# A short FFN part: two of its down blocks as a pair of seven products, and later joins of the query rows, in a float32 decoder layer on one core

## The chip, the cores and the metric

The kernel runs on one core of one Trainium2 chip. The core's engines are TensorE (PE, matmul; PEld is its weight load), VectorE (DVE), ScalarE (ACT), GpSimd (POOL) and SyncE (SP, which here only starts DMA transfers). The metric is the time of one execution on the device in microseconds; lower is better. A profile records one execution, instruction by instruction. A time of before or after is the median of several executions.

## The reference

One decoder layer in float32 on 256 tokens of width 2048: two token mixers (retention and a gated linear recurrence) that are merged, cross-attention to 256 memory tokens, and a gated FFN of width 5632 with a causal convolution of three taps. Cut to the two places that the change touches:

```python
def memory_cross_attention(hn, mem_n, w_q, w_k, w_v, w_o):
    q = (hn @ w_q).reshape(b, s, XA_HEADS, XA_HEAD_DIM)      # 4 heads of 512
    k = (mem_n @ w_k).reshape(b, m, XA_HEADS, XA_HEAD_DIM)
    v = (mem_n @ w_v).reshape(b, m, XA_HEADS, XA_HEAD_DIM)
    logits = einsum("bshd,bmhd->bhsm", q, k) * XA_HEAD_DIM ** -0.5
    o = einsum("bhsm,bmhd->bshd", softmax(logits), v).reshape(b, s, D_MODEL)
    return o @ w_o

def conv_gated_ffn(hn, w_up, conv_w, conv_b, w_down):
    up = causal_dwconv(hn @ w_up, conv_w, conv_b)            # 2048 -> 2 x 5632
    gate, val = split(up, 2)
    return (silu(gate) * val) @ w_down                       # 5632 -> 2048

h = h + conv_gated_ffn(rmsnorm(h, norm_ffn_w), ...)
return rmsnorm(h, final_norm_w)
```

## The kernel before

**Precision.** A float32 number is kept as a high part `hi`, which TensorE takes at its faster float32 rate, and a rest `lo`. A product is three matmuls: hi x hi, lo x hi, hi x lo.

**The weight stream.** All weights come in pieces of 1 MB (`raw`, 4 k-tiles of 128 rows by 512 columns), in an order that `weight_plan` fixes. `prefetch` takes the next unit of the stream: SP starts the load (L267), ACT casts `raw` to `hi` (L288), VectorE subtracts to get `lo` (L289). There are 6 `raw` buffers and 3 of `hi` and `lo`, and two units are prepared ahead of the one that PE works on. `units` hands the prepared units out and counts a step for each; `later(n, fn)` puts work at n steps from now, which is how side work is spread over the units. Within that, a scheduler sets each engine's order when the program is built; after that each engine works in its order and waits by semaphores. SP's queue is in order too: a load that waits for its buffer holds up what stands behind it.

**Plain blocks.** A block of 512 output columns by `gemm_n` is 24 matmuls of 128x512 for each unit: 2 tiles of rows (128 tokens each), 4 k-tiles, 3 terms (upper terms L364 and L365, lower term L371). `gemm_t` (L353) computes the transposed block, with weights as the stationary operand. Both accumulate in the `acc` pool, three accumulators of two 512-column halves in PSUM.

**Pairs.** `pair_products` computes two neighbouring blocks over 8 k-tiles with seven products of sums in place of eight (q1 to q7, 12 matmuls each), as in Strassen's and Winograd's method; k-tiles 8 to 15 go by direct units p0 to p3. The halves of the two accumulated tensors have the names x, z (one accumulator), y, u (second) and r, w (third). It needs sums of weight pieces, which stand in the slots A, B and C: q5 works on A plus a further piece, which a DMA on POOL's queue adds while loading; VectorE adds A+B, A+C (L294, L296). It also needs sums of the left operand's tiles (`sums`: four small VectorE steps, a cast, a subtraction). `pair_add` is the version that adds the products to the residual rows `hrow` (the `nat` tiles, L429).

**The FFN.** It goes in parts of 4, 4 and 3 blocks of 512 hidden features (`FF_PARTS`). For each hidden block two products with `ffn_w_up` give gate and value; `conv` applies the convolution (ACT L1314, VectorE L1316), `hidden` the gate (L1387 to L1389), and the result is split into planes `hid`. Then the part's down product adds to `hrow`. A part of four blocks has 16 k-tiles and takes two pairs; the last part has 12 k-tiles and takes four plain blocks (`down`). A gate or value block computed by `gemm_n` is turned by ACT copies (`rp`), an SP transpose (`d`, L781) and ACT copies that join the two 16-bit planes (`jp`, L766); the very last value block comes transposed from `gemm_t` and is scaled (`uz`, L548 and L679). In the last part SP loads the kept rows (`nat` from `fkept`, L1382); after each of blocks 0 to 2 `finish` squares and scales its rows for the final norm. The last block is worked out column by column, and the normed rows go out.

**The query rows.** Under `xa_w_q` the query blocks are stored (`qs`), and under `xa_w_k` they come back by a transposing load (`qs.load`, L801) and are joined and split (`qs[i]`: ACT L766 and L555, VectorE L556) before `softmax` needs them. The table with `later` times behind `turn_key` sets in which unit each load and each join is placed.

Of the kernel before, what the change touches and what calls it, by code (L numbers as in the profile page):

```python
# [14 lines left out]
ALU = mybir.AluOpType  # L15
# [49 lines left out]
def weight_plan():  # L65

    w0 = "w_in"
    plan = []
    v, u = O_V, O_V + 1024
    plan += [(w0, 0, NT, O_Q), (w0, 0, NT, v), (w0, 0, NT, O_K), (w0, 0, NT, v + BW), (w0, 0, NT, O_G, O_G + BW)]  # L70
    plan += [(w0, 0, NT, O_Q + BW), (w0, 0, NT, u, u + BW), (w0, 0, NT, O_K + BW)]
    plan += [(w0, 0, NT, O_G + 1024, O_G + 1024 + BW)]
    for b in range(4):
        plan += [(w0, 0, NT, c + b * BW) for c in (O_XR, O_YR)]
    for w, c, pairs in ((w0, O_GA, (0, 2)), (w0, O_GB, (0,)), ("w_proj_ret", 0, (0, 2))):
        plan += [(w, 0, NT, c + b * BW, c + (b + 1) * BW) for b in pairs]
        if len(pairs) == 1:
            plan += [(w, 0, NT, c + b * BW) for b in (2, 3)]
    plan += [("w_proj_rnn", 0, NT, b * BW) for b in range(4)]
    plan += residual_plan("w_mix_out")  # L80
    plan += [(w, 0, NT, b * BW, (b + 1) * BW) for w in ("xa_w_q", "xa_w_k") for b in (0, 2)]
    plan += residual_plan("xa_w_v")
    plan += residual_plan("xa_w_o")
    b0 = 0
    for nb_ in FF_PARTS:
        for b in range(b0, b0 + nb_):
            plan += [("ffn_w_up", 0, NT, c + b * BW) for c in ((0, FF) if b > b0 or b == 0 else (FF,))]
        if b0 + nb_ < sum(FF_PARTS):
            plan += [("ffn_w_up", 0, NT, (b0 + nb_) * BW)]
        if nb_ == 4:  # L90
            plan += [("ffn_w_down", b0 * BW, NT, b * BW, (b + 1) * BW) for b in (0, 2)]
        else:
            plan += [("ffn_w_down", b0 * BW, 4 * nb_, b * BW) for b in range(4)]
        b0 += nb_
    return plan

# [20 lines left out]
]  # L117


def entry_units(e):  # L120

    w, row, nk, cols = e[0], e[1], e[2], e[3:5]
    if len(cols) == 1:
        return [("p", None, "new", (w, tuple(row + (k + i) * P for i in range(KC)), cols[0])) for k in range(0, nk, KC)]
    out = []
    for kind, slot, a in PAIR_UNITS:
        if kind[0] == "p":
            out.append((kind, slot, "new", (w, tuple(row + (a[1] + i) * P for i in range(KC)), cols[a[0]])))
        elif a[0] == "sum":
            out.append((kind, slot, "sum", None))  # L130
# [26 lines left out]
def hybrid_layer(  # L157
# [92 lines left out]
    def prefetch(n):  # L250
        while len(ahead) < n and taken[0] < len(stream):
# [58 lines left out]
    def units(*e):  # L310

        assert plan[gemms[0]] == e, (gemms[0], plan[gemms[0]], e)
        gemms[0] += 1
        for _ in entry_units(e):
            prefetch(1)
            kind, parts = ahead.pop(0)
            prefetch(AHEAD)
            yield kind, parts
            step[0] += 1
            due = [p for p in pending if p[0] <= step[0]]  # L320
            pending[:] = [p for p in pending if p[0] > step[0]]
            for _, fn in due:
                fn()
# [60 lines left out]
                lower_n(a[:, tt, :], ops[tt], parts, k0 + KC >= nk)  # L384
        return a

    def pair_products(w, row, st, ss, c0, c1, out):
# [19 lines left out]
        e = (w, row, NT, c0, c1)  # L407
        for kind, parts in units(*e):
            if kind in rows:
                k0, *to = rows[kind]  # L410
# [12 lines left out]
            with tc.high_priority(URGENT):  # L423
                out(kind, x, z, yu, rw)

    def pair_add(w, row, st, ss, c0, c1, hs, late=False):

        def add(o, i, op=ALU.add):
            dve.tensor_tensor(out=o, in0=o, in1=i, op=op)  # L429

        def out(kind, x, z, yu, rw):
            h0, h1 = (hrow[i] for i in hs)
            if kind == "q1" and not late or kind == "q5" and late:
                add(h0[:, 0, :], x)
            if kind == "q5":
                later(3, lambda: add(h1, rw))
                later(4, lambda: add(h1, z[:, None, :].to_broadcast([P, 2, BW])))
            elif kind == "q6":
                add(h1[:, 0, :], x, ALU.subtract)
            elif kind == "q7":  # L440
                add(h0[:, 1, :], x)
                add(h1[:, 1, :], x, ALU.subtract)
            elif kind == "p3":
                add(h0, yu)

        pair_products(w, row, st, ss, c0, c1, out)

    def pair_out(w, st, ss, c0, r=None):

# [798 lines left out]
            later(5 + pr, lambda pr=pr: ks.append(split_pair(join_planes(d, pr))))  # L1248
        later(8, lambda: softmax([qs[2 * b], qs[2 * b + 1]], ks))

    for b, at in ((0, ((2, 6, 8), (6, 10, 12))), (2, ((3, 7, 9), (8, 12, 14)))):
        for i, (n, *joins) in enumerate(at):
            later(n, qs.load)
            for pr, m in enumerate(joins):
                later(m, lambda i=2 * b + 2 * i + pr: qs[i])
        for i, o in enumerate(pair_out("xa_w_k", ms, ms.sums, b * BW, rsms[0])):
            later(1 + 4 * i, lambda b=b + i, o=o: turn_key(b, o))
# [123 lines left out]
            hrow[b] = big([P, 2, BW], s="nat")  # L1381
            sp.dma_start(out=hrow[b], in_=fkept[n, b])  # L1382

    def hidden(gt, vl, pr, summed):
# [3 lines left out]
        dve.scalar_tensor_tensor(out=o, in0=th, scalar=1.0, in1=gt[:, cs, :], op0=ALU.add, op1=ALU.mult)  # L1388
# [22 lines left out]
    for part, nb_ in enumerate(FF_PARTS):  # L1411
# [3 lines left out]
        for b in range(b0, b0 + nb_):  # L1415
            gt, vl = big([P, 4, S], s="fg"), big([P, 4, S], s="fv")
            last = b + 1 == b0 + nb_
            if b0 and b == b0:
                sp.dma_start(out=gt, in_=gkept[part - 1])
            else:  # L1420
                up(0, b, (1, 2), lambda pr, z, b=b, gt=gt: conv(0, b, pr, z, gt))
            if last and final:
                later(0, lambda part=part: get_rows(part % 2, range(4)))

            def finish_up(pr, z, b=b, gt=gt, vl=vl, paired=paired):
                conv(FF, b, pr, z, vl)
                hidden(gt, vl, pr, paired)

            up(FF, b, None if last and final else (1, 2), finish_up)
        if not final:  # L1430
# [56 lines left out]
```

## Time and profile before

| | us |
|---|---|
| three executions | 1977.21, 1982.29, 1982.72 |
| their median | 1982.29 |
| the profiled execution | 1977.05 |
| its span | 1975.3 |
| PE busy in the span | 1961.2 |
| VectorE busy in the span | 1564.9 |
| ACT busy in the span | 1295.6 |
| POOL busy in the span | 43.2 |

The span is what the profiler saw of one execution, from the first to the last instruction; the time of that execution is 1.75 us longer. A row of a timeline has the start in us, the length in us, the engine, the line of the kernel, the operation, output and inputs, shapes, and a count; in brackets stands how long the engine had been idle before and what it waited for. Where instructions of an engine overlap, the distance from one start to the next tells what each costs. A row of the busy times by stretch has the stretch, its length, for each engine the busy time and the number of instructions, then the granted TensorE clock, the share of DMA busy time, and GB/s.

### The profile page before, as it was taken

How to read it: one execution, taken by the hardware profiler on the slowest of the kernel's cores; microseconds unless marked ns; L12 is line 12 of the kernel's file. 1: busy time of each engine (PE TensorE's matmuls, PEld its weight loads, DVE VectorE, ACT ScalarE, POOL GpSimd, SP SyncE). 2: the span in 40 equal slices, each digit the busy share in tenths (PEclk: the TensorE clock that was granted, in tenths of full speed). 3: DMA queues.
4: the chain of work that ended last, by engine and by line, in shares of the span. 5: the costliest groups of instructions: out<-in, count | busy, mean ns of one | idle time of the engine just before them, and what ended most of it. 6: DMA issues, size and time to landing. Idle time of an engine off the chain costs nothing. (4 is left out here: it accounts for less than half of the span.)

```text
span 1975.3 us, 23603 instructions
## 1 busy us (share of the span) xinstructions
PE 1961.2 (99%) x9264; PEld 1645.0 (83%) x9264; DVE 1564.9 (79%) x1546; ACT 1295.6 (66%) x1349; POOL 43.2 (2%) x52
## 2 busy tenths in 40 slices
PE   9999999999999999999999999999999999999998
PEld 8888888888888888888888888888888888888887
DVE  6988887889986886778888868777779676796775
ACT  6655656767667656667778767666765577655663
POOL 0000000000000000000000000000000000000000
PEclk9999999999999999999999999999999999999999
DMA  9675774655887776878998838867689677797671
GB/s 369 232 253 147 244 254 172 214 194 158 259 257 240 255 236 212 245 288 239 280 262 224 284 128 250 274 220 212 222 224 305 234 230 225 204 302 271 215 244 63
DMA packets 157598, 461.29 MB, mean 234 GB/s; under 512 B 88368, under 2 KB 93104, under 8 KB 109744
## 3 DMA queue, kind: packets, MB, share of 16 engines
q1 hardware_dynamic: 150208, 415.23, 60.0%
q0 software_dynamic: 5760, 41.95, 11.5%
q10 hardware_dynamic: 1520, 2.63, 0.4%
q8 instruction: 72, 1.18, 0.2%
q14 instruction: 38, 0.31, 0.0%
HBM read 422.01 MB, written 17.83 MB: 223 GB/s over the span
## 5 line engine op out<-in xcount | busy, mean ns | idle before, releaser
L289 DVE TENSOR_TENSOR lo<-raw,hi 128x2048 fp32r<-128x2048 f32 (+1 forms) x420 | 950.8, 2268 | 290.6 <-ACT hi L288 288.6
L288 ACT CAST hi<-raw 128x2048 fp32r<-128x2048 f32 (+1 forms) x418 | 792.2, 1901 | 479.7 <-PE acc L365 311.6
L364 PE MATMUL acc<-hi,s 128*128 128x512 f32 x2008 | 783.1, 390 | 0.4 <-ACT hi L288 0.2
L365 PE MATMUL acc<-hi,s 128*128 128x512 f32 x2008 | 781.6, 389 | 0.0
L371 PE MATMUL acc<-lo,s 128*128 128x512 f32 x2008 | 500.7, 389 | 0.0
L364 PEld LDWEIGHTS acc<-hi,s 128*128 128x128 f32 x2008 | 376.9, 188 | 78.4 <-ACT hi L288 0.6
L371 PEld LDWEIGHTS acc<-lo,s 128*128 128x128 f32 x2008 | 376.9, 188 | 78.3
L365 PEld LDWEIGHTS acc<-hi,s 128*128 128x128 f32 x2008 | 377.1, 188 | 77.6 <-DVE s L559 0.2
L353 PE MATMUL acc<-s,hi 128*128 128x512 f32 x832 | 201.9, 394 | 1.1 <-DVE hi L286 1.1
L353 PEld LDWEIGHTS acc<-s,hi 128*128 128x128 f32 x832 | 154.3, 189 | 31.8 <-issue 1.4
L766 ACT COPY jp<-d 128x512 uint16<-128x512 uint16 x152 | 108.4, 772 | 33.1 <-DMA d<-rp 33.1
L364 PE MATMUL acc<-hi,ss 128*128 128x512 f32 x320 | 125.9, 394 | 2.3 <-DVE nat L429 1.5
L365 PE MATMUL acc<-hi,ss 128*128 128x512 f32 x320 | 124.7, 390 | 0.0
L353 PEld LDWEIGHTS acc<-s,lo 128*128 128x128 f32 x832 | 108.0, 192 | 4.7 <-DVE lo L289 1.0
L353 PE MATMUL acc<-s,lo 128*128 128x256 f32 x832 | 111.1, 284 | 0.4 <-DVE lo L289 0.4
L371 PE MATMUL acc<-lo,ss 128*128 128x512 f32 x320 | 85.9, 390 | 0.0
L364 PEld LDWEIGHTS acc<-hi,ss 128*128 128x128 f32 x320 | 60.1, 188 | 17.4 <-DVE nat L429 3.0
L371 PEld LDWEIGHTS acc<-lo,ss 128*128 128x128 f32 x320 | 60.1, 188 | 12.6
L365 PEld LDWEIGHTS acc<-hi,ss 128*128 128x128 f32 x320 | 60.1, 188 | 12.1
L269 POOL DMA_DIRECT2D raw<-in_wall x40 | 35.2, 880 | 1555.6 <-DVE lo L289 925.1
L429 DVE TENSOR_TENSOR nat<-nat,acc 128x512 f32<-128x512 f32 (+1 forms) x49 | 44.0, 910 | 3.4 <-DMA nat<-in_x 1.7
L294 DVE TENSOR_TENSOR raw<-raw,raw 128x2048 f32<-128x2048 f32 x20 | 45.8, 2288 | 0.5
(232 smaller groups left out, 1249.1 us busy)
## 6 DMA issues: line engine op xcount, KB each, us to landing
raw<-in_wall SPq DMA_DIRECT2D x333, 1024.0 KB, 5.0
raw<-in_wall POOLq DMA_DIRECT2D x40, 1024.0 KB, 8.2
fkept<-nat SPq DMA_DIRECT2D x12, 512.0 KB, 8.0
nat<-fkept SPq DMA_DIRECT2D x12, 512.0 KB, 4.8
xt<-in_x_t SPq DMA_DIRECT2D x11, 256.0 KB, 7.8
raw<-in_wall SPq DMA_DIRECT2D x5, 512.0 KB, 8.2
nat<-in_x ACTq DMA_DIRECT2D x4, 512.0 KB, 9.8
ret<-hr SPq DMA_DIRECT2D x4, 512.0 KB, 4.8
```

What stands on the lines that cost most here:

```text
L269: pool.dma_start(out=raw, in_=src, accum_op=ALU.add)
L288: act.copy(hi[:, a:b], raw[:, a:b])
L289: dve.tensor_tensor(out=lo[:, a:b], in0=raw[:, a:b], in1=hi[:, a:b].bitcast(F32), op=ALU.subtract)
L294: dve.tensor_tensor(out=to, in0=to, in1=by, op=ALU.add)
L353: pe.matmul(a, part, sx, start=k == 0 and t == 0, stop=k == nk - 1 and t == 0, skip_group_check=True)
L364: pe.matmul(o, h, hi, start=start and kk == 0, stop=False, skip_group_check=True)
L365: pe.matmul(o, l, hi, start=False, stop=False, skip_group_check=True)
L371: pe.matmul(o, h, lo, start=False, stop=stop and kk == KC - 1, skip_group_check=True)
L429: dve.tensor_tensor(out=o, in0=o, in1=i, op=op)
L766: ins = act.copy(words(t)[:, :, :, 1 - i], d[:, i, 2 * pr : 2 * pr + 2, :])
```

## The change

There are two parts, and they touch places 800 us apart.

First, the down blocks 0 and 1 of the last FFN part become a pair. Since the part has 12 k-tiles and not 16, there is a list of units of its own, `SHORT_PAIR_UNITS`: seven products over k-tiles 0 to 7 and two direct units, p0 and p1, for k-tiles 8 to 11. POOL has no part in it. A unit `d` loads the fourth piece D into a `raw` buffer and does nothing else; the operation `sumd` has VectorE add D to slot A before q5 and to slot B before q7. The other two sums, A+B and A+C, are by VectorE as in the longer pair. The first product is added to `hrow` right after q1, not after q5 as in the longer pairs (`late` is not set here). The sums of `hid` are now made in the last part too. Blocks 2 and 3 stay as they were.

Second, the table for the query rows under `xa_w_k` has other times: first pair of heads, loads at 3 and 8 in place of 2 and 6, joins at 14, 15, 18 and 19 in place of 6, 8, 10 and 12; second pair, loads at 8 and 14 in place of 3 and 8, joins at 12, 13, 19 and 20 in place of 7, 9, 12 and 14.

```diff
+SHORT_PAIR_UNITS = [
+    ("q1", "A", ("new", 0, 0)),
+    ("q3", "B", ("new", 1, 1)),
+    ("d", "D", ("new", 0, 1)),
+    ("q5", "A", ("sumd",)),
+    ("q2", "C", ("new", 1, 0)),
+    ("q6", "A", ("sum",)),
+    ("p0", None, (1, 8)),
+    ("q7", "B", ("sumd",)),
+    ("q4", "A", ("sum",)),
+    ("p1", None, (0, 8)),
+]
...
@@ prefetch
+            if kind == "d":
+                sp.dma_start(out=raw, in_=src)
+                continue
+            if op == "sumd":
+                dve.tensor_tensor(out=raw, in0=raw, in1=held["D"], op=ALU.add)
...
@@ xa_w_k
-    for b, at in ((0, ((2, 6, 8), (6, 10, 12))), (2, ((3, 7, 9), (8, 12, 14)))):
+    for b, at in ((0, ((3, 14, 15), (8, 18, 19))), (2, ((8, 12, 13), (14, 19, 20)))):
         for i, (n, *joins) in enumerate(at):
             later(n, qs.load)
...
@@ hidden
-        if summed and len(hid_sums) < KC:
+        if len(hid_sums) < KC:
             hid_sums.append(sums(o, 0.5))
...
@@ the last part
         else:
-            for b in range(4):
+            pair_add("ffn_w_down", b0 * BW, hid, hid_sums, 0, BW, (0, 1), nk=4 * nb_)
+            for b in range(2):
+                finish(b)
+            for b in (2, 3):
                 down(b0, hid, b, final)
```

How this moves instructions shows best on VectorE from the last convolution on. Before, rows in the order in which VectorE works, from the second value half's scaling (`uz`, L679) to the add of block 0 (`nat`, L1327); `fv` is the value after its convolution, `fo` the gated product, `s` its split, `lo` a weight's rest:

```order
L679 TENSOR_TENSOR uz_14380<-uz_14380,rsb 128x512
L1388 TENSOR_SCALAR fo_14391<-ft_14390,fg_14013 128x512
L559 TENSOR_SCALAR s_14376<-fo_14372,s_14376 128x2x256
L1316 TENSOR_SCALAR fv_14014<-uz_14380,pf,fv_14014 128x255 x2
L1316 TENSOR_SCALAR fv_14014<-uz_14380,pf,fv_14014 128x254 x2
L289 TENSOR_TENSOR lo_14436<-raw_14433,hi_14435 128x2048
L1389 TENSOR_TENSOR fo_14391<-fo_14391,fv_14014 128x512
L289 TENSOR_TENSOR lo_14466<-raw_14463,hi_14465 128x2048
L559 TENSOR_SCALAR s_14395<-fo_14391,s_14395 128x2x256
L1327 TENSOR_TENSOR nat_14218<-nat_14218,acc_14402 128x1024
```

After, the same place; `raw_14306` is slot A, `raw_14354` B, `raw_14437` D and `raw_14458` C, `acc_14434` holds x and z, and L449 is the add to `hrow`:

```order
L700 TENSOR_TENSOR uz_14412<-uz_14412,rsb 128x512
L1410 TENSOR_TENSOR fo_14404<-fo_14404,fv_14030 128x512
L1409 TENSOR_SCALAR fo_14423<-ft_14422,fg_14029 128x512
L1337 TENSOR_SCALAR fv_14030<-uz_14412,pf,fv_14030 128x255 x2
L580 TENSOR_SCALAR s_14408<-fo_14404,s_14408 128x2x256
L1337 TENSOR_SCALAR fv_14030<-uz_14412,pf,fv_14030 128x254 x2
L316 TENSOR_TENSOR raw_14306<-raw_14306,raw_14354 128x2048
L1410 TENSOR_TENSOR fo_14423<-fo_14423,fv_14030 128x512
L449 TENSOR_TENSOR nat_14250<-nat_14250,acc_14434 128x512
L309 TENSOR_TENSOR lo_14461<-raw_14458,hi_14460 128x2048
L580 TENSOR_SCALAR s_14427<-fo_14423,s_14427 128x2x256
L309 TENSOR_TENSOR lo_14477<-raw_14306,hi_14476 128x2048
```

The add of q1's product stands behind the whole of the value convolution and the weight sum A+B, and ahead of the split of C. On PE, after, this is where q5 (into `acc_14434`, from A+D in `hi_14440`) follows the upper terms of q2 (into `acc_14435`); a wait for VectorE stands at its first matmul:

```order
L385 MATMUL acc_14435<-hi_14460,s_14107 128x512
L384 MATMUL acc_14435<-hi_14460,s_14163 128x512
L385 MATMUL acc_14435<-hi_14460,s_14163 128x512
L384 MATMUL acc_14434<-hi_14440,ss_13782 128x512 [waits DVE_49]
L385 MATMUL acc_14434<-hi_14440,ss_13782 128x512
```

Before, PE goes on there with the next unit of the same block, whose accumulator `acc_14402` nobody empties until the block's end:

```order
L371 MATMUL acc_14402<-lo_14277,s_13779 128x512 x2
L371 MATMUL acc_14402<-lo_14277,s_13827 128x512 x2
L364 MATMUL acc_14402<-hi_14324,s_14091 128x512 [waits Activation_49]
L365 MATMUL acc_14402<-hi_14324,s_14091 128x512
L364 MATMUL acc_14402<-hi_14324,s_14091 128x512
```

On SP, before, the two transposes that turn the last gate block (`d_14175`) stand behind five loads of down pieces, of which the last is `raw_14463`:

```order
L267 DMA raw_14274<-in_wall 128x2048
L267 DMA raw_14322<-in_wall 128x2048
L267 DMA raw_14403<-in_wall 128x2048
L267 DMA raw_14433<-in_wall 128x2048
L267 DMA raw_14463<-in_wall 128x2048
L781 DMA_TRANSPOSE d_14175<-rp_14172 128x8x128 x2
```

After, they stand behind six, with D among them and p1's piece `raw_14558` last:

```order
L287 DMA raw_14306<-in_wall 128x2048
L287 DMA raw_14354<-in_wall 128x2048
L278 DMA raw_14437<-in_wall 128x2048
L287 DMA raw_14458<-in_wall 128x2048
L287 DMA raw_14492<-in_wall 128x2048
L287 DMA raw_14558<-in_wall 128x2048
L802 DMA_TRANSPOSE d_14207<-rp_14204 128x8x128 x2
```

One more raw load is ahead of the transposes. In the middle of the kernel, under `xa_w_k`, the order on ACT changes between the first head's probabilities (`pT`) and the second head's (`prob`). Before, `jp_8417` being a joined query:

```order
L1230 COPY pT_8361<-sm_8356 128x512
L288 COPY hi_8389<-raw_8387 128x2048
L766 COPY jp_8417<-d_8183 128x512 x2
L760 COPY rp_8363<-o_7942 128x2x512 x2
L288 COPY hi_8460<-raw_8191 128x2048
L555 COPY s_8420<-jp_8417 128x2x256
```

After:

```order
L1251 COPY pT_8347<-sm_8342 128x512
L781 COPY rp_8349<-o_7924 128x2x512 x2
L787 COPY jp_8373<-d_8175 128x512 x2
L308 COPY hi_8381<-raw_8379 128x2048
L576 COPY s_8376<-jp_8373 128x2x256
L308 COPY hi_8448<-raw_8183 128x2048
```

The copies `rp` and `jp` now stand ahead of the weight cast that was ahead of them.

More of the change, by code (lines that the diff above doesn't have):

```diff
@@ L92, in weight_plan @@
         else:
-            plan += [("ffn_w_down", b0 * BW, 4 * nb_, b * BW) for b in range(4)]
+            plan += [("ffn_w_down", b0 * BW, 4 * nb_, 0, BW)]
+            plan += [("ffn_w_down", b0 * BW, 4 * nb_, b * BW) for b in (2, 3)]
         b0 += nb_
@@ L125, in entry_units @@
     out = []
-    for kind, slot, a in PAIR_UNITS:
+    for kind, slot, a in PAIR_UNITS if nk == NT else SHORT_PAIR_UNITS:
         if kind[0] == "p":
             out.append((kind, slot, "new", (w, tuple(row + (a[1] + i) * P for i in range(KC)), cols[a[0]])))
-        elif a[0] == "sum":
-            out.append((kind, slot, "sum", None))
+        elif len(a) == 1:
+            out.append((kind, slot, a[0], None))
         else:
@@ L313, in units @@
         gemms[0] += 1
-        for _ in entry_units(e):
+        for _ in range(sum(u[0] != "d" for u in entry_units(e))):
             prefetch(1)
@@ L385, in gemm_n, with pair_products @@
         return a
-    def pair_products(w, row, st, ss, c0, c1, out):
+    def pair_products(w, row, st, ss, c0, c1, out, nk=NT):
         xz, yu, rw = acc(), acc(), acc()
@@ L406, in pair_products @@
         names = {"q1": "x", "q2": "y", "q3": "r", "q4": "u", "q5": "z", "q6": "x", "q7": "x"}
-        e = (w, row, NT, c0, c1)
+        e = (w, row, nk, c0, c1)
         for kind, parts in units(*e):
@@ L424, in pair_products, with pair_add @@
                 out(kind, x, z, yu, rw)
-    def pair_add(w, row, st, ss, c0, c1, hs, late=False):
+    def pair_add(w, row, st, ss, c0, c1, hs, late=False, nk=NT):
         def add(o, i, op=ALU.add):
@@ L434, in out @@
                 add(h0[:, 0, :], x)
+            short = nk < NT
             if kind == "q5":
@@ L442, in out @@
                 add(h1[:, 1, :], x, ALU.subtract)
-            elif kind == "p3":
+            elif kind == ("p1" if short else "p3"):
                 add(h0, yu)
-        pair_products(w, row, st, ss, c0, c1, out)
+        pair_products(w, row, st, ss, c0, c1, out, nk)
     def pair_out(w, st, ss, c0, r=None):
@@ L1382, in get_rows, with hidden @@
             sp.dma_start(out=hrow[b], in_=fkept[n, b])
-    def hidden(gt, vl, pr, summed):
+    def hidden(gt, vl, pr):
         cs = slice(2 * pr, 2 * pr + 2)
@@ L1423, in hybrid_layer, with finish_up @@
                 later(0, lambda part=part: get_rows(part % 2, range(4)))
-            def finish_up(pr, z, b=b, gt=gt, vl=vl, paired=paired):
+            def finish_up(pr, z, b=b, gt=gt, vl=vl):
                 conv(FF, b, pr, z, vl)
-                hidden(gt, vl, pr, paired)
+                hidden(gt, vl, pr)
             up(FF, b, None if last and final else (1, 2), finish_up)
```

## The prediction

> **What bounds the kernel now.** I read the page's first part, then the chain of waits, the busy time by stretches, and the timeline of each engine around the last FFN part.
>
> ```profile
> span 1975.3 us, 23603 instructions
> ...
> PE 1961.2 (99%) x9264; PEld 1645.0 (83%) x9264; DVE 1564.9 (79%) x1546; ACT 1295.6 (66%) x1349; POOL 43.2 (2%) x52
> ```
>
> PE is the bound: only 14 us of the span are not matmul. So a change gains what it takes off PE, and loses what it makes PE wait. The chain of waits (start, us, engine, work) around the last part:
>
> ```profile
> 1878.24 11.13 PE acc L353 x64
> 1889.39 1.17 ACT jp L766 x2
> ...
> 1942.80 1.81 PE acc L371 x8
> 1948.24 1.81 PE acc L371 x8
> ```
>
> Two weight units end 5.44 us apart (1948.24 - 1942.80). A unit is 24 matmuls of 128x512 (2 row tiles, 4 k-tiles, 3 terms), so one costs 0.227 us. The other row I need is 1889.39: there a `hi` buffer of the weight stream comes free. By stretches (length, then busy time of PE, PEld, DVE, ACT, POOL, granted clock, DMA):
>
> ```profile
> 1085.00:1095.00 10.00, 9.10 (x43) 7.27 (x42) 9.50 (x11) 9.62 (x12) 0.00 (x0) 1.00 1.03 247
> ...
> 1875.00:1889.00 14.00, 14.00 (x79) 12.22 (x78) 7.72 (x9) 6.64 (x6) 0.00 (x0) 1.00 0.77 215
> 1889.00:1914.00 25.00, 25.00 (x126) 21.07 (x124) 22.34 (x32) 18.76 (x23) 0.00 (x0) 1.00 0.63 239
> 1914.00:1930.00 16.00, 15.79 (x70) 12.85 (x70) 10.70 (x8) 7.31 (x8) 0.00 (x0) 1.00 0.72 263
> 1930.00:1950.00 20.00, 20.00 (x90) 16.57 (x89) 10.01 (x7) 8.80 (x8) 0.00 (x0) 1.00 0.00 0
> ```
>
> PE is full in nearly all of the last part, but between 1889 and 1914 VectorE is full too, 22.34 of 25 us: it finishes the last convolution and gate while it splits weights. The change puts its new VectorE work and its new PSUM adds into just that stretch, so I work through it instruction by instruction.
>
> **The tail, part by part.** Matmuls: two blocks of three units are 2 x 72 = 144; seven products of 12 and two direct units of 24 are 132. Gain 12 x 0.227 = 2.7 us. The weights loaded stay at 6 MB (six pieces). Units split go from 6 to 9, three more casts on ACT and subtractions on VectorE, and four weight sums are added to VectorE. What VectorE's pieces cost:
>
> ```profile
> 1883.87 2.29 DVE L289 TENSOR_TENSOR lo<-raw,hi 128x2048 fp32r<-128x2048 f32 x1 [2.57 <-ACT hi L288]
> ...
> 1892.35 2.29 DVE L289 TENSOR_TENSOR lo<-raw,hi 128x2048 fp32r<-128x2048 f32 x1 [1.70 <-ACT hi L288]
> 1894.56 1.66 DVE L1316 SCALAR_TENSOR_TENSOR fg<-jp,pf,fg 128x255 f32<-128x255 f32 x4
> 1896.14 0.68 DVE L1304 TENSOR_TENSOR jp<-jp,rsb 128x512 f32<-128x512 f32 x1
> 1896.74 2.28 DVE L289 TENSOR_TENSOR lo<-raw,hi 128x2048 fp32r<-128x2048 f32 x1
> ...
> 1900.52 0.68 DVE L548 TENSOR_TENSOR uz<-acc,c 128x512 f32<-128x512 f32 x1
> 1901.12 0.68 DVE L1388 SCALAR_TENSOR_TENSOR fo<-ft,fg 128x512 f32<-128x512 f32 x1
> ```
>
> Start to next start, back to back, a split takes 2.20 us (1892.35 to 1894.56), a convolution step 0.395 (four in 1.58), a 128x512 step 0.60. A weight sum has the size of a split, and POOL has no part in it:
>
> ```profile
> L294 DVE TENSOR_TENSOR raw<-raw,raw 128x2048 f32<-128x2048 f32 x20 | 45.8, 2288 | 0.5
> ```
>
> so 2.20 us as well. PE reaches the first down matmul at the same time in both kernels:
>
> ```profile
> 1900.30 0.40 PE L364 MATMUL acc<-hi,s 128*128 128x512 f32 x1
> ```
>
> On VectorE the order now is: split of q1, A+=D, two `jp`, split of q3, eight gate steps, `uz` of the first half, split of q5, `uz`, `fo`, `uz` of the second half, four value steps, `uz`, two `fo`, four value steps with `s` between them, A+=B, `fo`, and only then the add that takes q1's product out of PSUM (`nat<-nat,acc`). q5 is written into the other half of q1's accumulator, and its first matmul waits for that add. This is the wait the change creates. Counted: 5 large steps x 2.20 = 11.0; 16 convolution steps x 0.395 = 6.3; 11 steps of 0.60 = 6.6; the add 0.6; and about 0.7 of short waits for ACT: 25.2 us. It starts when q1's `hi` is there: buffer free at 1889.4, cast 1.9 us (row 1890.42 below), so 1891.35. The add ends at 1916.55. PE needs q1, q3 and the upper part of q2 before q5: 32 x 0.227 = 7.25 us after 1900.35, plus two smaller waits. q3 and q2 take the accumulators that the last `ffn_w_up` block leaves by the two `uz` steps; by the same count those end at 1903.5 and 1907.55, while PE is there at 1903.05 and 1906.35: 0.55 and 1.3 us. So PE stands at q5 from 1909.5 to 1916.7: **7.2 us**. Nothing else is ready on PE, since q2's lower terms and q6 are queued behind q5.
>
> After it VectorE has split C (2.2), `s` (0.6), split of q6 (2.2), of p0 (2.2), A+=C (2.2), B+=D (2.2), which ends at 1928.2; ACT casts B by 1930.2. PE has 52 matmuls (11.8 us) from 1916.7 and would want q7 at 1928.45: another 1.8 us. From there a q unit's two splits and one sum fit; the two `finish` steps and blocks 2 and 3 stand as before with PE full (20.00 of 20 us above). Before's own idle there is 0.2 us (15.79 of 16).
>
> Sum of the tail: 0.55 + 1.3 + 7.2 + 1.8 - 0.2 - 2.7 = **+7.9 us**. Bounds: -2.9 if all four waits were covered, +11 to +13 if the planes below come late.
>
> SP's queue also moves. p1's raw load, which waits for a buffer, now stands ahead of the two transposes that bring the last gate's planes:
>
> ```profile
> 1881.15 5.24 SPq L781 DMA_TRANSPOSE d<-rp  x2
> 1886.44 2.00 SPq L1382 DMA_DIRECT2D nat<-fkept  x4
> ```
> ```profile
> 1888.53 2.03 ACT L766 COPY jp<-d 128x512 uint16<-128x512 uint16 x3 [4.72 <-DMA d<-rp]
> 1890.42 1.90 ACT L288 CAST hi<-raw 128x2048 fp32r<-128x2048 f32 x1
> ```
>
> The buffer is freed by the split that starts at 1883.87 and ends at 1886.1, so the transposes go from 1881.15 to about 1886.5, `jp` from 1888.5 to about 1893, its second copy to 1894.3. VectorE wants it at 1895.9 (behind A+=D), so 1.6 us are to spare, and I cost it at nothing; each us beyond that is a us on the q5 wait. The `nat` loads behind them land well before the add at 1916.
>
> The sums of the hidden planes are now made in the last part too (four 0.28 us steps, one of 0.68 on VectorE, one cast on ACT, four times):
>
> ```profile
> L504 DVE TENSOR_TENSOR sm<-oc x4: 281/284/293, 1128.5 to 1149.2; 128x128 f32<-128x128 f32 x4
> ...
> L510 DVE TENSOR_TENSOR ss<-sm,ss x4: 683/684/684, 1130.9 to 1152.0; 128x512 fp32r<-128x512 f32 x4
> ```
>
> 1.8 us each, ahead of the stretch; the one nearest falls where VectorE is busy 7.72 of 14 us. Nothing.
>
> **The middle.** The kept query rows' transposes and joins go later under `xa_w_k`. Before has one short hole there:
>
> ```profile
> 1090.05 0.84 PE L371 MATMUL acc<-lo,ss 128*128 128x512 f32 x3
> 1091.80 0.30 PE L1222 MATMUL sm<-cid,prob 128*128 128x128 f32 x1 [0.90 <-DVE prob L1215]
> ```
> ```profile
> 1076.10 1.94 ACT L288 CAST hi<-raw 128x2048 fp32r<-128x2048 f32 x1
> 1077.91 1.44 ACT L766 COPY jp<-d 128x512 uint16<-128x512 uint16 x2
> 1079.38 1.99 ACT L760 COPY rp<-o 128x1024 uint16<-128x1024 uint16 x2
> ...
> 1084.81 1.92 ACT L288 CAST hi<-raw 128x2048 fp32r<-128x2048 f32 x1 [1.11 <-PE acc L365]
> ```
>
> The most it can gain is that hole, 1.06 us (1090.05 to 1091.80 less three matmuls). Against it, the new order on ACT has the two `jp` and the two `rp` ahead of a weight cast that was ahead of them: 3.4 us later (1.44 + 1.99), in a stretch where ACT and VectorE are busy 9.6 and 9.5 of 10 us. ACT had 1.1 us to spare before the next cast but one (last row), so PE can lose up to 2.3. Between -1.1 and +2.3 I take the middle, **+0.6**, since the same engines are as full before as after and only the order differs.
>
> Total 7.9 + 0.6 = +8.5 us: 1977.05 us of the profiled execution becomes 1985.6. The median of the runs shown is 1982.29, 5.2 above it; the difference is the same, so 1990.8, rounded to 1991.
>
> **Rivals.** (1) PE runs cold after the q5 wait. At the start, with PE not yet long busy, its matmuls go at half the pace (0.42 us from a 128x512 to the next, against 0.23 later):
>
> ```profile
> 7.17 0.63 PE L353 MATMUL acc<-s,hi 128*128 128x512 f32 x1
> 7.59 0.63 PE L353 MATMUL acc<-s,lo 128*128 128x256 f32 x2
> ...
> 12.08 0.39 PE L353 MATMUL acc<-s,hi 128*128 128x512 f32 x1
> 12.31 0.28 PE L353 MATMUL acc<-s,lo 128*128 128x256 f32 x1
> ```
>
> If 7 us of idle bring this back for a stretch as long as 3.5 to 7 us, half of that, 1.8 to 3.5 us, is lost, of which the 1.8 before q7 are slack, as VectorE sets q7's time: +0 to 1.7, so 1991 to 1992.5. Against it: the trace has no hole of 7 us, and nothing that shows how long an idle PE keeps its pace. The Trainium skill ("TensorE: Matmul & The Clock Gate", Part 1: The HAM clock gate) says that TensorE's clock falls to half after an idle window of about 3.4 us and returns after as long a busy one. Its rule is that of this rival and agrees with the start's pace; the price above doesn't use its figure.
>
> (2) The planes come late: the transposes land over 1.6 us later than worked out. They took 5.24 us to issue and landed 2.1 us behind that, in a stretch with DMA at 0.63 to 0.77; with one more weight load beside them 2 to 4 us more is possible. Then +1 to +2.5: 1992 to 1993.5.
>
> (3) The other side: VectorE's backlog is covered. The q5 wait vanishes if q1's add is done by 1909.4, 7.2 us earlier than I work out; that takes a start of VectorE's list at 1884, with the `hi` buffer free 7 us earlier, or a wait on something earlier than that add. Then the tail gains 2.7 less what is left of 1.3 + 1.8, and the middle up to 1.1: 1978.5 to 1982. The row 1889.39 speaks against it.
>
> **How the numbers follow.** 0.3% is 5.9 us, about what a measurement of this kernel can tell from no change. As summed (1988 to 1994): 0.45. Cold PE: 0.25. Late planes: 0.12. Covered: 0.18. The first three are slower by over 0.3% when the sum holds within 3 us; I take 0.11 off them for a q5 wait of 4 us or less, or for the 5.2 us between execution and median falling the other way. So slower 0.71, same 0.25, and faster 0.04, since no more than 4 us can be gained on the median. The range reaches from 1982 (half of the covered case, or the profiled execution's own level less 4) to 1996 (late planes and cold PE together).
>
> **What would show it.** After: PE waits about 7 us for VectorE's `nat<-nat,acc` near 1909 to 1917, at a q unit's first matmul; about 1.8 us ahead of q7 near 1928; block 2 begins some 8 us later. 12 matmuls less of 128x512. In the middle, near 1060 to 1130, PE waits of under 1 us each. A PE gap below 3 us at q5 would make the forecast wrong, as would a pace of 0.42 for tens of us after it.

## The result and the profile after

| | us |
|---|---|
| before, beside the changed kernel | 1981.64 (4 runs, 1977.21 to 1982.72) |
| the changed kernel | 1995.19 (4 runs, 1992.71 to 1996.09) |
| ratio | 1.0078, 95% interval 1.0055 to 1.0101 |
| a second time, against before on that chip | 1993.84 (5 runs) against 1979.01 (21 runs), ratio 1.0074, 1.0060 to 1.0088 |
| the changed kernel's profiled execution, its span | 1996.09, 1994.2 |

The kernel became slower by some 14 to 15 us. The prediction had 8.5 us. The median itself, 1995.19, lies just inside its range of 1982 to 1996; taken against the median that the prediction started from, 1.0078 x 1982.29 is 1997.8, above it. The sign was right, the size was not.

The first part of the page after the change, against the lines in the prediction:

```profile
span 1994.2 us, 23628 instructions
...
PE 1963.0 (98%) x9252; PEld 1644.2 (82%) x9252; DVE 1589.2 (80%) x1578; ACT 1302.4 (65%) x1356; POOL 43.2 (2%) x52
```

PE has its 12 matmuls less and yet is busy 1.8 us longer, in a span that is 18.9 us longer. So there are new waits, and some matmuls were slower. Busy times by stretch, the same columns as in the prediction:

```profile
1889.00:1914.00 25.00, 23.44 (x134) 20.34 (x132) 19.10 (x24) 17.71 (x20) 0.00 (x0) 1.00 0.72 235
1914.00:1930.00 16.00, 8.14 (x27) 6.06 (x28) 16.00 (x22) 7.30 (x11) 0.00 (x0) 0.76 0.00 0
1930.00:1950.00 20.00, 20.00 (x84) 16.29 (x84) 17.93 (x11) 10.32 (x6) 0.00 (x0) 0.93 0.68 254
```

Between 1914 and 1930 VectorE is busy without a gap and PE half of the time, and the clock that TensorE was granted is 0.76, then 0.93; before it was 1.00 in each of these stretches. PE's timeline at that place:

```profile
1914.00 0.50 PE L384 MATMUL acc<-hi,ss 128*128 128x512 f32 x1 [1.56 <-DVE uz L569]
...
1918.10 0.47 PE L384 MATMUL acc<-hi,s 128*128 128x512 f32 x1 [1.08 <-DVE uz L569]
...
1919.79 0.40 PE L385 MATMUL acc<-hi,s 128*128 128x512 f32 x1
1926.96 0.79 PE L384 MATMUL acc<-hi,ss 128*128 128x512 f32 x1 [6.78 <-DVE nat L449]
1927.55 0.63 PE L385 MATMUL acc<-hi,ss 128*128 128x512 f32 x1
1927.98 0.63 PE L384 MATMUL acc<-hi,ss 128*128 128x512 f32 x1
...
1933.39 0.40 PE L384 MATMUL acc<-hi,ss 128*128 128x512 f32 x1
1933.62 0.39 PE L385 MATMUL acc<-hi,ss 128*128 128x512 f32 x1
```

The third wait is q5's, for the add of q1's product, 6.95 us by the starts (1919.79 to 1926.96, less one matmul of 0.23). Behind it matmuls follow at 0.43 us until about 1932.7: the 16 from 1926.96 to 1933.39 take 6.4 us, where 3.6 is normal.

But these matmuls stand 9.2 us late before any of that (the first down matmul is at 1909.53, not 1900.30). That came from the middle, under `xa_w_k` and `xa_w_v`, where PE had three waits of note:

```profile
1089.45 0.50 PE L384 MATMUL acc<-hi,ss 128*128 128x512 f32 x1 [0.76 <-ACT o L478]
...
1100.92 0.50 PE L384 MATMUL acc<-hi,ss 128*128 128x512 f32 x1 [2.68 <-ACT hi L308]
...
1132.84 0.74 PE L542 MATMUL sm<-ps,v 128*128 128x256 f32 x4 [3.56 <-ACT v L591]
```

By the starts these waits are 0.92, 2.84 and 3.73 us, and behind the last one some matmuls again start 0.43 us apart (granted clock 0.72 between 1132 and 1138), about 1.5 us lost.

To compare kernels I cut the span at three starts in PE's timeline. "Middle" is from the first logits (`sm<-s,s`) to the first down matmul of the last part, "tail" from there to the first matmul of the last block:

| | first logits | first down | last block | middle | tail |
|---|---|---|---|---|---|
| before | 1060.2 | 1900.3 | 1949.9 | 840.1 | 49.6 |
| changed | 1059.6 | 1909.5 | 1968.8 | 849.9 | 59.3 |
| changed, second time | 1059.5 | 1905.1 | 1964.3 | 845.6 | 59.2 |

Two losses, then, some 800 us apart: 9.7 us in the tail, nearly the same both times, and 5.5 to 9.8 us in the middle. The experiments take them one at a time.

### The profile page after: what moved, and what is told of

It reads as the page before. It is cut to its first block, busy times and chain, and to the rows that moved or that the text cites. A ratio compares the mean times of both kernels' runs of the same rounds, so it can differ in the third digit from the quotient of the medians.

```text
span 1994.2 us, 23628 instructions
## 1 busy us (share of the span) xinstructions
PE 1963.0 (98%) x9252; PEld 1644.2 (82%) x9252; DVE 1589.2 (80%) x1578; ACT 1302.4 (65%) x1356; POOL 43.2 (2%) x52
## 3 DMA queue, kind: packets, MB, share of 16 engines
q10 hardware_dynamic: 1520, 2.63, 0.4%
## 5 line engine op out<-in xcount | busy, mean ns | idle before, releaser
L384 PE MATMUL acc<-hi,ss 128*128 128x512 f32 x336 | 133.6, 398 | 14.0 <-DVE nat L449 8.0
L385 PE MATMUL acc<-hi,ss 128*128 128x512 f32 x336 | 132.0, 393 | 0.0
L391 PE MATMUL acc<-lo,ss 128*128 128x512 f32 x336 | 91.4, 393 | 0.2 <-DVE lo L309 0.2
L384 PEld LDWEIGHTS acc<-hi,ss 128*128 128x128 f32 x336 | 63.6, 189 | 31.5 <-DVE nat L449 9.9
L385 PEld LDWEIGHTS acc<-hi,ss 128*128 128x128 f32 x336 | 63.7, 190 | 12.8
L449 DVE TENSOR_TENSOR nat<-nat,acc 128x512 f32<-128x512 f32 (+1 forms) x56 | 50.2, 908 | 2.9 <-DMA nat<-in_x 1.6
## 6 DMA issues: line engine op xcount, KB each, us to landing
nat<-in_x ACTq DMA_DIRECT2D x4, 512.0 KB, 10.5
```

What stands on the lines that cost most here:

```text
L384: pe.matmul(o, h, hi, start=start and kk == 0, stop=False, skip_group_check=True)
L385: pe.matmul(o, l, hi, start=False, stop=False, skip_group_check=True)
L391: pe.matmul(o, h, lo, start=False, stop=stop and kk == KC - 1, skip_group_check=True)
```

## The middle: what the late loads collide with

ACT stood still there for 7.7 us, waiting for a transfer. Its row, and those of SP's and POOL's queues ahead of it:

```profile
1098.97 1.90 ACT L308 CAST hi<-raw 128x2048 fp32r<-128x2048 f32 x1 [7.68 <-DMA raw<-in_wall]
```
```profile
1081.06 1.85 SPq L822 DMA_TRANSPOSE d<-qs  x1
1089.52 0.33 SPq L287 DMA_DIRECT2D raw<-in_wall  x1
1091.31 10.50 SPq L802 DMA_TRANSPOSE d<-rp  x2
```
```profile
1081.20 0.88 POOL L289 DMA_DIRECT2D raw<-in_wall  x1 [19.81 <-DVE raw L316]
```

The cast is that of slot B for q7 in the second `xa_w_k` pair, to which POOL's adding load brings the fourth piece. POOL issued it 0.14 us behind the last query load, which the change had moved here from 1047.8. From 1070 to 1100, what was issued and how many us it took to land (last number), changed kernel and before:

```profile
raw<-in_wall POOLq DMA_DIRECT2D x1, 1024.0 KB, 17.7
d<-qs SPq DMA_TRANSPOSE x1, 18.4
```
```profile
raw<-in_wall POOLq DMA_DIRECT2D x1, 1024.0 KB, 8.4
```

And the stretch from 1080 to 1100, changed and before (the last two columns are the DMA share and GB/s):

```profile
1080.00:1100.00 20.00, 17.39 (x88) 13.89 (x86) 12.06 (x12) 10.73 (x13) 0.88 (x1) 1.00 1.15 126
```
```profile
1080.00:1100.00 20.00, 19.10 (x98) 16.03 (x97) 18.23 (x17) 18.03 (x22) 0.88 (x1) 1.00 0.92 232
```

The DMA engines are about full in both, but in the changed kernel they move 126 GB/s and not 232.

Transposes come in small pieces: of the packets in this stretch 3840 of 4032 are under 512 B, and before 4272 of 4711. The Trainium skill ("DMA: Bandwidth & Descriptors", Specifications) says that transfers under 512 B miss the full rate. The trace agrees: in the changed kernel between 1076 and 1081, where the queue of SP moves only such packets, 0.27 MB take 29.1% of the engines' time, 186 GB/s for the time taken; in run qs_one (below) between 1047 and 1056, where nearly all packets are larger, 3.49 MB take 97.9%, 396 GB/s.

But there are no fewer small packets before, so they alone don't explain the difference. Before, the last query load stood 33 us ahead of POOL's load, and two transposes of another block stood next to it:

```profile
1047.82 6.58 SPq L801 DMA_TRANSPOSE d<-qs  x1
...
1081.40 7.78 SPq L781 DMA_TRANSPOSE d<-rp  x2
```
```profile
1080.99 0.88 POOL L269 DMA_DIRECT2D raw<-in_wall  x1 [22.38 <-DVE raw L296]
```

There POOL issued 0.41 us ahead of the transposes, and they took 7.8 us to issue; now the query load is 0.14 us ahead of POOL, takes 1.9 us to issue, and the same 144 packets of POOL's load take 45.9% of the engines' time and not 28.6%. So which of the two is first differs, and POOL's weights land 9.3 us later. (Part of the lower rate is another effect: SP's next transposes took 10.5 us to issue and not 3.3, so the weight loads that stand behind them were issued from 1101.9 on, not 1094.6.)

PE waits for POOL's weights, and all that ACT has queued behind that cast comes late, at its end the split of the values for attention (`v`).

### Experiment qs_only: the query times alone

```diff
 before.py
-    for b, at in ((0, ((2, 6, 8), (6, 10, 12))), (2, ((3, 7, 9), (8, 12, 14)))):
+    for b, at in ((0, ((3, 14, 15), (8, 18, 19))), (2, ((8, 12, 13), (14, 19, 20)))):
```

> The query rows' new times alone, with plain blocks in the last part. If the middle's loss comes from them, PE waits 2.8 and 3.7 us near 1098 and 1129 and the time is 9 to 10 us over the kernel before. By the prediction, which priced only the order of ACT's copies, +0.6 us (range -1.1 to +2.3).

Measured 1984.53 us against 1978.42, ratio 1.0033 (1.0016 to 1.0050): 6.1 us. Middle 849.1, tail 49.4. Landing times as above, and the wait for `v`:

```profile
raw<-in_wall POOLq DMA_DIRECT2D x1, 1024.0 KB, 15.2
...
d<-qs SPq DMA_TRANSPOSE x1, 15.9
```
```profile
1130.63 1.22 PE L521 MATMUL sm<-ps,v 128*128 128x256 f32 x4 [3.57 <-ACT v L570]
```

The 3.7 us wait is there, the 2.8 us one is 0.35 us here: the adding load came 2.5 us sooner. The profiled execution lost 9 us in the middle, the median of twelve 6. The loss is the new times', and the prediction's +0.6 is refuted.

### Experiment qs_joins: old loads, late joins

```diff
-    for b, at in ((0, ((2, 6, 8), (6, 10, 12))), (2, ((3, 7, 9), (8, 12, 14)))):
+    for b, at in ((0, ((2, 14, 15), (6, 18, 19))), (2, ((3, 12, 13), (8, 19, 20)))):
```

> Loads of the query rows at the old times (2, 6, 3, 8), joins at the new ones (14, 15, 18, 19, 12, 13, 19, 20), plain blocks. Theory loads: the late transposing loads fill the DMA queues ahead of weights, so with old loads both long waits go and the time is within 3 us of before. Theory joins: the late ACT copies stand ahead of the value split, so the 3.7 us wait at the first value product stays, with 1.5 us of slow matmuls behind it: 5 us over before.

Measured 1980.67 us against 1978.42, ratio 1.0017 (0.9986 to 1.0047), middle 843.0.

```profile
raw<-in_wall POOLq DMA_DIRECT2D x1, 1024.0 KB, 8.0
```
```profile
1126.19 0.74 PE L521 MATMUL sm<-ps,v 128*128 128x256 f32 x4 [0.72 <-ACT v L570]
```

With the loads back, the adding load lands in 8.0 us and the wait for `v` falls to 0.9. The late joins alone lengthen the middle by 2.9 us in the profile, with waits of 1.05, 0.93 and 0.88 us by the starts. That is what I had bounded at 2.3.

### Experiment qs_one: only the last load and its joins late

```diff
-    for b, at in ((0, ((2, 6, 8), (6, 10, 12))), (2, ((3, 7, 9), (8, 12, 14)))):
+    for b, at in ((0, ((2, 6, 8), (6, 10, 12))), (2, ((3, 7, 9), (14, 19, 20)))):
```

> Plain blocks, the query rows' old times except for the last load and its two joins (14, 19, 20 in place of 8, 12, 14). Theory last load: the load issued near 1081 us takes the DMA engines for some 16 us, the two transposes of the key planes and the next weights come late behind it, and the time is 4 to 6 us over before, as with the whole table. Theory joins: only two of eight joins are late, and the time is within 2 us of before.

Measured 1979.02 us against 1978.12, ratio 0.9999 (0.9978 to 1.0021), middle 840.7: no loss. By my words that speaks for the joins. The rows show another thing:

```profile
1078.03 7.33 SPq L801 DMA_TRANSPOSE d<-qs  x1
```
```profile
1078.05 0.87 POOL L269 DMA_DIRECT2D raw<-in_wall  x1 [20.45 <-DVE raw L296]
```
```profile
raw<-in_wall POOLq DMA_DIRECT2D x1, 1024.0 KB, 9.5
```

Here POOL's load is issued 0.02 us behind the query load and not 0.14, SP needs 7.3 us to issue its load and not 1.9, and POOL's weights land in 9.5 us. It is still the adding load whose landing decides, only it wasn't the late one.

### Experiment qs_last: all late but the last load

```diff
-    for b, at in ((0, ((2, 6, 8), (6, 10, 12))), (2, ((3, 7, 9), (8, 12, 14)))):
+    for b, at in ((0, ((3, 14, 15), (8, 18, 19))), (2, ((8, 12, 13), (9, 19, 20)))):
```

> Plain blocks, the query rows' new times with one entry put back: the last load at 9 in place of 14, so that it no longer is issued next to POOL's adding load near 1081 us. Theory adding load: POOL's load lands in 8 to 10 us again (15.2 and 17.7 with the new table), the 3.7 us wait at the first value product shrinks to about 1, no slow pace, and the time is 1 to 3 us over before. Theory joins: the late joins alone make it, the wait stays above 3 us, and the time is 5 to 7 us over before.

Measured 1980.03 us against 1979.01, ratio 1.0006 (0.9989 to 1.0022), middle 842.2.

```profile
raw<-in_wall POOLq DMA_DIRECT2D x1, 1024.0 KB, 8.0
```
```profile
1126.37 0.74 PE L521 MATMUL sm<-ps,v 128*128 128x256 f32 x4 [0.73 <-ACT v L570]
```

One number in the table, 14 or 9, makes the difference between 6 us and 1. That the loss comes from where the last load stands, together with a late landing of POOL's adding load (15.2 us against 8.0), is thereby shown. How the one delays the other is read from the traces alone, and qs_one says that the place 14 by itself is not enough.

## The tail: VectorE's backlog and a cold PE

### Experiment pair_only: the pair alone

```diff
 after.py
-    for b, at in ((0, ((3, 14, 15), (8, 18, 19))), (2, ((8, 12, 13), (14, 19, 20)))):
+    for b, at in ((0, ((2, 6, 8), (6, 10, 12))), (2, ((3, 7, 9), (8, 12, 14)))):
```

> The pair alone, with the query rows' old times. If the two parts are independent, the tail loses what it lost in the changed kernel (first down matmul to last block: 59.4 against 49.8 us), so about 10 us over the kernel before, and the middle is as before. If the late middle made part of the tail's loss, the pair alone costs less, near the 7.9 us of the prediction's sum.

Measured 1988.19 us against 1978.42, ratio 1.0047 (1.0027 to 1.0068): 9.8 us. Middle 839.9, tail 59.6. Its wait at q5:

```profile
1916.97 0.79 PE L384 MATMUL acc<-hi,ss 128*128 128x512 f32 x1 [6.79 <-DVE nat L449]
```

The two parts add up: 0.47% and 0.33% are 0.80%, against 0.78% and 0.74% for the changed kernel, and each leaves the other's stretch as it was before.

### Experiment pair_late: q1's add behind q5

```diff
 pair_only
-            pair_add("ffn_w_down", b0 * BW, hid, hid_sums, 0, BW, (0, 1), nk=4 * nb_)
+            pair_add("ffn_w_down", b0 * BW, hid, hid_sums, 0, BW, (0, 1), True, nk=4 * nb_)
```

> The pair with the old query times, and q1's product added to the rows after q5 and not before it, as the longer pairs do. Theory add: q5 no longer waits (7 us gone), and the time is 3 us or less over before. Theory backlog: VectorE's work of some 25 us ahead is the bound, and the wait moves to q6, which needs A+B summed and cast: some 4 to 5 us are left there, and the time is 5 to 7 us over before, 3 to 5 under the pair alone.

Measured 1991.58 us against 1978.42, ratio 1.0070 (1.0041 to 1.0099), tail 59.7.

```profile
1924.16 2.08 PE L391 MATMUL acc<-lo,s 128*128 128x512 f32 x4 [7.25 <-DVE lo L309]
```

q5 doesn't wait any more, but the same 7 us now stand one step later, at the lower terms of q2, for the split of C. The add only was where VectorE's list happened to be felt. For the backlog I had expected 5 to 7 us over before and the wait at q6. It is 13.2 us with a wide interval (the tail is pair_only's, 59.6 us there), and the place was wrong; but the wait moved and did not go, as the theory says.

### Experiment pair_nosums: without the four weight sums

```diff
 pair_only
-            if op == "sumd":
-                dve.tensor_tensor(out=raw, in0=raw, in1=held["D"], op=ALU.add)
...
-            if after:
+            short = taken[0] > len(stream) - 16
+            if after and short:
+                after.pop()
+            if after:
...
-            if kind == "q5":
+            if kind == "q5" and not short:
```

> The pair with the old query times and without its four weight sums on VectorE (the result of blocks 0 and 1 is then not the product; the time is that of the rest). Two sums of 2.2 us stand ahead of the add that q5 waits for. Theory backlog: the 6.9 us wait at q5 falls by 4.4 to about 2.5, which is too short for the slow pace behind it (2.8 us), and the time is some 4 to 6 us under the pair alone, 3 to 6 over before. Theory add (the wait is a matter of where the add stands): the wait stays above 5 us.

Measured 1985.05 us against 1978.12, ratio 1.0028 (1.0006 to 1.0051), tail 56.0.

```profile
1909.95 0.50 PE L385 MATMUL acc<-hi,ss 128*128 128x512 f32 x1 [2.14 <-DVE uz L570]
1915.62 0.47 PE L385 MATMUL acc<-hi,s 128*128 128x512 f32 x1 [1.28 <-DVE uz L570]
1920.10 0.50 PE L385 MATMUL acc<-hi,ss 128*128 128x512 f32 x1 [2.40 <-DVE nat L450]
```
```profile
1912.00:1930.00 18.00, 14.31 (x50) 10.75 (x49) 18.00 (x22) 11.06 (x11) 0.00 (x0) 0.83 0.21 70
```

The wait at q5 falls from 6.95 to 2.56 us, by 4.4, two sums of 2.2: VectorE's backlog is the cause. The tail shrank by 3.6 us only. I had expected no slow pace behind so short a wait, and that was wrong: it came behind the first wait and behind the third (granted clock 0.83).

### Experiment pair_warm: matmuls to fill the waits

```diff
 pair_only, pair_products
+            if nk < NT and kind == "q2":
+                idle = small()
+                hi = parts[0][0][:, 0, :]
+                for _ in range(64):
+                    pe.matmul(idle[:, 0, :], hi[:, 0:P], hi[:, 0:S], start=True, stop=True)
```

> The pair with the old query times and 64 more matmuls of 128x256 (7.6 us in all, their results unused) ahead of q2 and of q5, where PE waits for VectorE. Theory cold PE: PE is no longer idle for long, the matmuls after the wait go at 0.23 us and not 0.43 (2.8 us), but part of that is slack ahead of q7, so the time is 1 to 3 us under the pair alone. Rival (the slow pace has another cause, the waits for VectorE): the pace stays 0.43 and the time is the same or longer.

Measured 1987.41 us against 1978.12, ratio 1.0057 (1.0030 to 1.0084), which can't be told from the pair alone; tail 58.6 against 59.6.

```profile
1919.52 6.39 PE L447 MATMUL sm<-hi 128*128 128x256 f32 x52
1926.37 0.50 PE L384 MATMUL acc<-hi,ss 128*128 128x512 f32 x1 [0.46 <-DVE nat L454]
1926.70 0.39 PE L385 MATMUL acc<-hi,ss 128*128 128x512 f32 x1
1926.93 0.40 PE L384 MATMUL acc<-hi,ss 128*128 128x512 f32 x1
...
1939.97 0.50 PE L384 MATMUL acc<-hi,ss 128*128 128x512 f32 x1 [1.52 <-ACT hi L308]
```

The pace behind the wait is 0.23 us at once. What that gains is given back in part at q7 (last row, 1.7 us by the starts), which waits for B+D: the slack that the prediction put at 1.8. So the slow pace is idle PE's, and its net price here is 1.0 us by the tails of one profile each; the 1 to 3 us that I expected on the median don't show.

### Experiments pair_12, pair_12_pool and pair_12_pool_qs: the pair where VectorE has room

```diff
 pair_only: pair_12
...
-            pair_add("ffn_w_down", b0 * BW, hid, hid_sums, 0, BW, (0, 1), nk=4 * nb_)
-            for b in range(2):
-                finish(b)
-            for b in (2, 3):
-                down(b0, hid, b, final)
+            down(b0, hid, 0, final)
+            pair_add("ffn_w_down", b0 * BW, hid, hid_sums, BW, 2 * BW, (1, 2), nk=4 * nb_)
+            for b in (1, 2):
+                finish(b)
+            down(b0, hid, 3, final)
...
 pair_12: pair_12_pool
-    ("d", "D", ("new", 0, 1)),
-    ("q5", "A", ("sumd",)),
+    ("q5", "A", ("add", 0, 1)),
...
-    ("q7", "B", ("sumd",)),
+    ("q7", "B", ("add", 0, 1)),
...
 pair_12_pool: pair_12_pool_qs
-    for b, at in ((0, ((2, 6, 8), (6, 10, 12))), (2, ((3, 7, 9), (8, 12, 14)))):
+    for b, at in ((0, ((2, 6, 8), (6, 10, 12))), (2, ((3, 7, 9), (14, 19, 20)))):
```

> Old query times, block 0 plain, blocks 1 and 2 as the pair, block 3 plain: the same work in another order, so that VectorE's gate and convolution lie beside block 0's 16 us of matmuls. Theory backlog: the waits at q3, q2 and q5 go, no slow pace, and the time is within 2 us of before, or 1 to 3 under it if all 2.7 us of saved matmuls come through. Rival (the pair is bound by VectorE wherever it stands: 9 splits and 4 sums take 29 us of its 30): 3 to 6 us over before.

> Old query times, blocks 1 and 2 as the pair behind a plain block 0, and the two sums with D by POOL's adding loads, as in the longer pairs, in place of VectorE (1 MB more is loaded). VectorE has 4.4 us less to do. Theory VectorE: the holes of 5.4 us that block 0 in front left shrink to 2 or less, without slow pace, and from the first down matmul to the last block it takes 48 us or less (49.6 before, 54.8 with VectorE's sums); the time is 1 to 3 us under before. Rival (adding loads land late): 2 to 5 us over before.

> The same with the last query load and its joins at the new times (14, 19, 20), the only part of that table that left no loss: if both hold, 1 to 4 us under before; the middle from the first logits to the FFN as before, 441 us.

Measured: pair_12 1984.39 us against 1978.12, ratio 1.0032 (1.0011 to 1.0053), tail 54.8. pair_12_pool 1985.57 against 1979.01, 1.0035 (1.0022 to 1.0048), tail 56.0. pair_12_pool_qs 1988.71 against 1979.01, 1.0051 (1.0035 to 1.0066), middle 847.6, tail 56.9. Waits of pair_12, then of pair_12_pool:

```profile
1915.76 0.50 PE L384 MATMUL acc<-hi,s 128*128 128x512 f32 x1 [1.15 <-DVE s L579]
...
1934.81 0.50 PE L383 MATMUL acc<-hi,ss 128*128 128x512 f32 x1 [2.02 <-ACT hi L307]
1947.05 0.50 PE L383 MATMUL acc<-hi,ss 128*128 128x512 f32 x1 [1.28 <-DVE nat L448]
```
```profile
1927.33 0.50 PE L382 MATMUL acc<-hi,ss 128*128 128x512 f32 x1 [2.18 <-ACT hi L306]
...
1934.97 0.50 PE L382 MATMUL acc<-hi,ss 128*128 128x512 f32 x1 [2.01 <-ACT hi L306]
```

With block 0 in front the 7 us wait is gone, and 4.8 of the pair's 10 us come back. But the rival holds: four smaller waits (1.3, 0.5, 2.2 and 1.4 us by the starts), with 1.8 us of slow matmuls behind the third, eat the 2.7 us and more. Taking the D sums off VectorE did not help, my expectation of 48 us was wrong: POOL's load may begin only when the slot's first use is split, and lands 7.9 us (median of the two) later, with the cast still to come, so PE waits for the casts of q5 and q7 instead. No placement of the pair that was run beats the kernel before.

pair_12_pool_qs has the table of qs_one, which cost nothing there, and its profiled execution loses 7 us in the middle; its median is 3.1 us above pair_12_pool's. Its rows:

```profile
1079.38 2.59 SPq L820 DMA_TRANSPOSE d<-qs  x1
```
```profile
1079.51 0.88 POOL L287 DMA_DIRECT2D raw<-in_wall  x1 [20.59 <-DVE raw L314]
```
```profile
raw<-in_wall POOLq DMA_DIRECT2D x1, 1024.0 KB, 17.5
```

POOL's load came 0.13 us behind the query load and landed in 17.5 us, where it came 0.02 us behind and landed in 9.5. That this tenth of a microsecond decides, by which transfer gets into the DMA queues first, fits all profiles (0.14 us behind: 13.3, 15.2 and 17.7; before and in the six runs of a pair with the old query times, 0.39 to 0.41 us ahead of two transposes: 8.2 to 8.4). SP's issue time fits as well: 7.3 us in qs_one, as for the transposes before (7.8), and 1.9 to 2.6 where POOL's load was late. But each is one execution, and no run tested the order by itself.

### The changed kernel again

> The changed kernel once more, beside the others. If its two parts add up, its median is 14 to 18 us over before (9.8 for the pair alone and 6.1 for the query times alone), and the profile again has 9 to 10 us in the tail and 2 to 10 in the middle.

Measured 1993.84 us against 1979.01: 14.8 us, ratio 1.0074 (1.0060 to 1.0088). Tail 59.2, middle 845.6, with the adding load landing in 13.3 us.

## Why the prediction was wrong in size

- **PE is the bound, VectorE's new work falls into a full stretch, the wait is q5's.** Right. The wait was put at 7.2 us and is 6.95, at the matmul named; the second, at q2, 1.3 and 1.24. That q5's is so near is in part luck: with the middle's 9.23 us taken off, PE was there at 1910.8 and not 1909.5, and q5 began at 1917.7 and not 1916.7.
- **q3's wait, 0.55 us.** It is 1.7. The planes of the gate came 1.2 us later than worked out (ACT's `jp` at 1903.43, 9.23 us of it from the middle, against "about 1893"). Most of that is a slip in the working: transposes that start 5.35 us later (1886.5 for 1881.15) bring `jp` from 1888.5 to 1893.9, which leaves 0.7 us to spare and not 1.6. VectorE idled 0.34 and 1.07 us for `jp` and for the cast behind it. That is the mechanism of the late-planes rival, in small; its condition, over 1.6 us late, was not met. (The prediction's 0.55 and 1.3 are 0.45 and 1.2 by the figures beside them, which changes little.)
- **1.8 us ahead of q7.** Not there in the changed kernel: the slow matmuls took that time up. It is there (1.7) in pair_warm, where they are not slow.
- **Rival 1, PE runs cold.** It came, with 2.8 us lost on 16 matmuls, and 1.0 net of the slack, inside the 0 to 1.7 given. It had a chance of 0.25; it should have been in the sum. The tail is then 1.7 + 1.2 + 6.95 + 2.8 - 0.4 (before's waits by the starts) - 2.7 = 9.6 us, measured 9.7, predicted 7.9.
- **The middle, +0.6 us, bounded by -1.1 and +2.3.** This step failed. It is 5.5 us of the miss, the tail 1.8. It priced the moved joins by ACT's copies and gave the moved transposing loads nothing: neither what they take of the DMA engines, nor what they stand next to. The trace had the rows for it: SP's four `d<-qs` issues, of up to 6.6 us each, and POOL's adding load at 1081, 8.4 us to landing in a stretch with a DMA share of 1.03. What the runs showed in its place: the moved last load, issued 0.14 us ahead of POOL's, goes with a landing 5 to 9 us later, and PE waits for what stands behind it. Measured +6.1 us on the median, 5 to 10 in the profiles.
- **The other side.** No cover for the backlog appeared; the start of VectorE's list at 1889.4 plus a cast, which spoke against it, was right.
- **Level.** 5.2 us were put on the profiled execution to get to a median of three. With 21 to 35 runs of before its median was 1978.1 to 1979.0, so most of that was chance. The difference doesn't depend on it.

## What to carry to other kernels

When a step with a DMA is moved, price the DMA at its new place first: what is issued within a microsecond of it, on any queue, and which of those landings somebody waits for. A saving of matmuls on a full PE is paid from other engines; add up their instructions between the last free moment and the first use, and if that list is longer than PE's work in the same stretch, the difference comes back as a wait; here a later add only moved it, and room ahead of the pair took away about half of the loss. And count a longer PE wait, here from about 2 us on, with the slow matmuls that may follow it.

## What the runs showed of the hardware

The slow pace comes after shorter waits than I had thought of. It followed waits of 6.95, 7.41, 4.31 and 3.73 us, but also of 2.03, 2.30 and 2.56 us in pair_nosums, of 2.18 us in pair_12 and pair_12_pool, and of 2.59 us in pair_12_pool_qs, while 2.84 us in the changed kernel, 2.63 in pair_warm, 2.35 in pair_12_pool and 2.03 in pair_only left none behind. So between 2.0 and 2.9 us it is open, and the length alone doesn't decide. The slow stretches lasted 2 to 6 us, and behind the shorter waits most set in late: behind the third wait of pair_nosums, which ends at 1920.10, the first matmuls are still 0.23 us apart, and 0.43 us starts at 1921.62. The Trainium skill ("TensorE: Matmul & The Clock Gate", Part 1: The HAM clock gate) gives an idle window of about 3.4 us that runs freely; a free-running window could explain why equal waits differ, but waits of 2.0 to 2.6 us are shorter than that window, and the runs decide.

The transposing load of the query rows (256 rows of 1024 two-byte numbers, 0.5 MB) landed in 7.6 us before (median of four), and in 11.3 to 18.4 us where it was issued next to POOL's adding load. That adding load of 1 MB landed in 13.3 to 17.7 us where it was issued 0.13 to 0.14 us behind the query load, and in 8.0 to 9.5 us in all other runs.
